# Transposing keys, gated outputs and probabilities from float32r copies in a hybrid GLA/attention encoder

## The chip, the cores and the metric

The kernel runs on one core of a Trainium2 chip. The metric is the time of one execution on the device, in microseconds (us). A core has five engines with a queue of instructions each: PE (TensorE, matrix products, whose weight loads are shown apart as PEld), DVE (VectorE), ACT (ScalarE), POOL (GpSimd) and SP (SyncE, which here only issues DMAs). Each engine works through its queue in order; they wait for each other through semaphores. A DMA is issued on the queue of an engine and then runs by itself.

## The reference

Two residual layers over 512 tokens of width 1024, in float32. Layer 0 mixes the tokens by gated linear attention (GLA), layer 1 by grouped-query softmax attention with rotary positions; each is followed by a gated MLP with a width-3 convolution. What matters here:

```python
# GLA, each of 4 heads, in both directions, in chunks of the tokens
kv_chunk = einsum('bhncd,bhncv->bhndv', k * exp(b_end - b), v)   # needs k with tokens on the contracted axis
...
o = rmsnorm(o, norm_w) * silu(g)                                  # the gated outputs
return o @ w_out
# attention, each of 8 query heads, in blocks of 128 queries
s = einsum('bkgqd,bksd->bkgqs', q_blk, k) * scale
p = softmax(s)                                                    # the probabilities
return einsum('bkgqs,bksd->bkgqd', p, v)                          # needs p with keys on the contracted axis
```

## The kernel before, in words

Activations are kept with features on the 128 partitions and the 512 tokens along them. Every large product is made of three products in float32r (`mm3`, L264 to L268): high part by high part, high by low, low by high. Both factors are split into a rounded float32r part (an ACT copy) and the rest (a DVE subtraction). Weights come as 1 MB tiles (`raw`, two buffers) on SP's queue, issued in `Weights.make` (L118), and are split there (L143, L144); a load waits until the tile two before it has been split.

The stages follow each other: GLA, MLP 0, attention, MLP 1. A tile framework puts the waits in, and a scheduler of its own orders the instructions on each engine, within what the program and the pools of buffers allow.

**GLA.** For each head h, `proj(h + 1)` (48 products of 512 columns) is written ahead of `core(h)`; after head 3's core there is none. `core(h)` does in order: `end`, the keys times a decay, for both directions (POOL, L482); their transposes by PE into the bank `kt`, three blocks of 128x128 a direction (L489), and an ACT copy into `kts` (L491); the products `in` (L501); the products `kv` of `kts` with `v` (L524), with ACT and DVE steps that chain them into states `sa` and `sb` (L525, L527); the outputs `o` (L548). Then ACT squares the outputs (L552, `junk`), DVE and POOL make a power of their sums (L198, L200, `ors`), and DVE multiplies outputs, this factor and the gate into the tiles `g` (L555). `tail(h)` transposes eight blocks of `g` by PE (L561, bank `tp`) and splits them into `oT` (L563, L564), the input of the output product `op` (L323). It is called inside the core of the next head; `tail(3)` comes after twelve steps of `op`.

**Attention.** 32 blocks (8 heads by 4 blocks of queries) go through a loop written out by hand: at step t it calls `scores(t)` (product `s`, its maximum, the exponential into a tile `p` of the tag "t", L784), then steps of generators that the lists `Q_STEPS`, `Q_READY` and `O_STEPS` assign to this t (projections of later query pairs, and the output product), then `turn(t - LAG)` (four transposes of `p` into the bank `pt`, L802, split into `pth` and `ptl`, L805 and L806), then `shares(t)` (`p` times the reciprocal of its sum, L789, L790), and every second step `mix` for the block `t - LAG2` (the products `po` with v, L266 to L268). LAG is 4 and LAG2 is 6. The banks for `s` are two, those for transposes (`pt`) are two, and the tag "t" has six buffers.

All transposes are `pe.transpose(out, in, ident)` with float32 tiles and a float32 identity.

Of the kernel before, what the change touches and what calls it, by code (L numbers as in the profile page):

```python
# [8 lines left out]
F32 = mybir.dt.float32  # L9
# [3 lines left out]
ALU = mybir.AluOpType  # L13
# [15 lines left out]

GATE_STEPS, GATE_LAG = (1, 3, 5, 7, 10, 12, 15, 17), 2  # L30

LAGS = (4, 6)

Q_STEPS = {1: (0, (4,) * 4), 2: (4, (3, 3, 2, 2, 2, 2, 2)), 3: (11, (2,) * 8)}
Q_READY = {1: (4, (3, 3, 2, 1, 1, 0, 1)), 2: (11, (3, 2, 2, 1, 1, 1, 0, 1)), 3: (19, (3, 2, 2, 1, 1, 1, 0, 1))}

O_STEPS = (22, 23, 25, 27, 29, 31, 32, 33, 34, 35, 36, 37)


PC_NORM = 0  # L40
# [6 lines left out]
def hybrid_encoder_kernel(  # L47
# [123 lines left out]
        sync.dma_start(raw[c // 4][:, r], w_vg[c // 4, :, r])  # L171
        W.raw[id(w_vg), c // 4] = raw[c // 4]

    ident = cp.tile([P, P], F32, name="ident")
    make_identity(nc, ident)

    two = tmp("u", "two")
    dve.memset(two[:, :P], 2.0 ** -5)
# [13 lines left out]
    def rsqrt_eps(src, w, n, scale=None, tag="tiny"):  # L192

        t = tiny(w, n, tag)
        if scale is None:
            dve.tensor_scalar(t, src, EPS, None, ALU.add)
        else:
            dve.tensor_scalar(t, src, scale, EPS, ALU.mult, ALU.add)  # L198
        r = tiny(w, n, tag)
        pool.tensor_tensor(r, t, halfneg[:, :w], ALU.pow)  # L200
        return r
# [141 lines left out]
    def gla(norm, nxt):  # L343
# [128 lines left out]

        def core(h, kqt, then):
            ends = big(F32, "end")
            ends = [ends[:, :S], ends[:, S:]]
            for d in range(2):
                e, f = EK[h, d], ends[d]
                dve.tensor_tensor(e[:, S:], e[:, S:], kqt[:, S:], ALU.mult)
                dve.tensor_tensor(e[:, :S], e[:, :S], kqt[:, :S], ALU.mult)
                sup = slice(0, 3) if d == 0 else slice(1, 4)  # L480
                v3 = lambda t: t.rearrange("p (s t) -> p s t", t=P)[:, sup, :]
                pool.tensor_tensor(v3(f), v3(e[:, S:]), FK[h, d][:, sup].rearrange("p (s o) -> p s o", o=1)  # L482
                                   .to_broadcast([P, 3, P]), ALU.mult)

            orders, keys = ([0, 1, 2], [3, 2, 1]), []
            for d, order in enumerate(orders):
                kt = bank("pt", "kt")
                for i, s in enumerate(order):
                    pe.transpose(kt[:, i * P : (i + 1) * P], ends[d][:, s * P : (s + 1) * P], ident)  # L489
                kts = tmp("t", "kts")  # L490
                act.activation(kts[:, : 3 * P], kt[:, : 3 * P], AF.Copy)  # L491
                keys.append(kts)

            at = tmp("t", "at")
            banks = []
            for d in range(2):
                e = EK[h, d]
                b = bank("acc" if h == GH - 1 else "s", "in")
                for s in range(NT):
                    o = s * P  # L500
                    mm(b[:, o : o + P], e[:, S + o : S + o + P], e[:, o : o + P], start=True, stop=True)  # L501
                banks.append(b)
            act.activation(at, banks[0], AF.Copy)

            def upper():
                dve.copy_predicated(at3, msk, banks[1].rearrange("p (s c) -> p s c", c=P))

            at3 = at.rearrange("p (s c) -> p s c", c=P)
            msk = smask.rearrange("p (o c) -> p o c", o=1).to_broadcast([P, NT, P])

            st = {}
            hs = slice(h * DV, (h + 1) * DV)
            for d, order in enumerate(orders):
                kts = keys[d]
                sa = tmp("t", "sa")
                sb = tmp("t", "sb") if d == 0 else st["b"]
                st["b"] = sb
                step = 1 if d == 0 else -1
                kv = bank("acc", "kv")
                kv2 = bank("po", "kv2")  # L520
                place = [kv[:, :DV], kv[:, DV:], kv2[:, :DV]]
                slot = [sa[:, :DV], sa[:, DV:], sb[:, d * DV : (d + 1) * DV]]
                for i, s in enumerate(order):
                    mm(place[i], kts[:, i * P : (i + 1) * P], v[s][:, hs], start=True, stop=True)  # L524
                act.activation(slot[0], place[0], AF.Copy)  # L525
                for i in (1, 2):
                    last = dve.scalar_tensor_tensor(slot[i], slot[i - 1], FK[h, d][:, order[i] : order[i] + 1],  # L527
                                                    place[i], ALU.mult, ALU.add)
                for i, s in enumerate(order):
                    st[d, s + step] = slot[i]  # L530
                if d == 0:
                    with tc.issue_after(last.ins) if h == GH - 1 else ExitStack():
                        upper()
            if then is not None:
                then()

            oss = tiny(4, "oss")
            og = []
            for s in range(NT):
                if s % 2 == 0:  # L540
                    bo = bank("s", "o")
                po = bo[:, (s % 2) * DV : (s % 2 + 1) * DV]
                parts = [(at[:, s * P : (s + 1) * P], v[s][:, hs])]
                for d in range(2):
                    if (d, s) in st:
                        parts.append((EK[h, d][:, s * P : (s + 1) * P], st[d, s]))
                for i, (l, r) in enumerate(parts):
                    mm(po, l, r, start=i == 0, stop=i == len(parts) - 1)  # L548
                og.append(po)
            for s in range(NT):  # L550
                junk = tmp("sq", "junk", DV)
                act.activation(junk, og[s], AF.Square, accum_out=oss[:, s : s + 1])  # L552
            ors = rsqrt_eps(oss, NT, "ors", 1.0 / DV)
            for s in range(NT):
                dve.scalar_tensor_tensor(g[s][:, hs], og[s], ors[:, s : s + 1], g[s][:, hs], ALU.mult, ALU.mult)  # L555

        def tail(h):
            for c in (2 * h, 2 * h + 1):
                tp = bank("pt", "tp")
                for s in range(NT):  # L560
                    pe.transpose(tp[:, s * P : (s + 1) * P], g[s][:, c * P : (c + 1) * P], ident)  # L561
                t = pair("xhl", 8, F32R, "oT")
                act.activation(t[:, :S], tp, AF.Copy)  # L563
                dve.tensor_tensor(t[:, S:], tp, t[:, :S].bitcast(F32), ALU.subtract)  # L564
                oh[c] = (t[:, :S], t[:, S:])
# [70 lines left out]
    def attention(norm, nxt):  # L636
# [90 lines left out]
        def qpair(i, tag="acc"):  # L727
            head, sc = yield from roped(1 + i, PC_QK, float(HD), "qsc", tag)
            for e in range(2):
                y = head(e)  # L730
                yield
                t = big(F32R, "q")
                split(y, t)
                heads[2 * i + e] = (t, sc, e)
                yield
# [51 lines left out]
        def shares(h, j):  # L787
# [2 lines left out]
            dve.tensor_scalar(p, p, rc, None, ALU.mult)  # L790
            probs[h, j] = p

        def turn(h, j):

            hf, i = divmod(j, 2)
            if i == 0:
                pts[h, hf] = tuple(big(F32R, n).rearrange("p (k q) -> p k q", q=256) for n in ("pth", "ptl"))
            ph3, pl3 = pts[h, hf]
            p = probs.pop((h, j))
            tp = bank("pt", "pt")  # L800
            for k in range(NT):
                pe.transpose(tp[:, k * P : (k + 1) * P], p[:, k * P : (k + 1) * P], ident)  # L802
            isl = slice(i * P, (i + 1) * P)
            tp3 = tp.rearrange("p (k q) -> p k q", q=P)
            act.activation(ph3[:, :, isl], tp3, AF.Copy)  # L805
            dve.tensor_tensor(pl3[:, :, isl], tp3, ph3[:, :, isl].bitcast(F32), ALU.subtract)  # L806
# [15 lines left out]
        LAG, LAG2 = LAGS  # L822
        blocks = [(h, j) for h in range(QH) for j in range(NT)]
        osteps = out_steps(w_aout, oh, nxt)
        plan = collections.defaultdict(list)
        for i in range(1, QH // 2):
            g = qpair(i)
            for first, counts in (Q_STEPS[i], Q_READY[i]):
                for t, n in enumerate(counts):
                    plan[first + t] += [g] * n  # L830
        for t in O_STEPS:
            plan[t].append(osteps)
        for t in range(len(blocks) + LAG2):
            if t < len(blocks):
                scores(*blocks[t])
            for g in plan[t]:
                next(g, None)
            if LAG <= t < len(blocks) + LAG:
                turn(*blocks[t - LAG])
            if t < len(blocks):  # L840
                shares(*blocks[t])
            if t >= LAG2:
                h, j = blocks[t - LAG2]
                if j % 2 == 1:
                    mix(h, j // 2)
# [88 lines left out]
```

## Time and profile before

| | |
|---|---|
| time, median of 3 runs | 1133.47 us (1133.27 to 1133.87) |
| time of the profiled execution | 1133.16 us |
| its span, first to last instruction | 1131.4 us |
| PE busy | 1125.7 us, 99% |
| DVE, ACT, POOL busy | 690.1, 482.1, 76.0 us |
| HBM read and written | 100.34 MB, 2.10 MB |
| transposes of `pt`, `tp`, `kt` | 128, 32, 24 |

A row of a group names the line, the engine, the operation, output and inputs, the shape and the count; behind the bar stand the busy time of all and the mean duration of one in ns, then the idle time ahead of them. A row of the timeline begins with the start and the length in us, and one of the chain of waits' pieces likewise. A row of the waits names who waited for whom, the total in us, how often, and the longest. A row of one tile gives the shortest, middle and longest duration in ns. A row of a window gives its length, then the busy time of PE, PEld, DVE, ACT and POOL, the granted PE clock, the share of the DMA engines and GB/s. A row of a DMA gives the count, the size and the median us from issue to landing.

### The profile page before, as it was taken

To read this page: it belongs to the slowest core of one execution; us is meant where nothing else is said; L and a number is where in the kernel's file an instruction comes from. 1 tells how busy PE (TensorE), PEld (TensorE's weight loads), DVE (VectorE), ACT (ScalarE), POOL (GpSimd) and SP (SyncE) were. 2 spreads that over 40 slices of the span, in tenths; PEclk is the share of its full clock that TensorE was granted. 3 is DMA by queue.
4 is the path that set the end of the run, shared out by engine and by line. 5 is a ranking of instruction groups with operands and counts; after the bars stand their busy time and mean duration, and the time that the engine had idled before them with its cause. 6 is when DMAs were issued, how large, how long until landed. Compare 5 with 4: busy or idle time off the path is not lost.

```text
span 1131.4 us, 12991 instructions
## 1 busy us (share of the span) xinstructions
PE 1125.7 (99%) x5260; PEld 939.2 (83%) x5260; DVE 690.1 (61%) x996; ACT 482.1 (43%) x690; POOL 76.0 (7%) x66
## 2 busy tenths in 40 slices
PE   9999999999999999999999999999999999999998
PEld 7888888888888888888888888888888888888887
DVE  6787563677777777633325589766777777762221
ACT  5564232444444444422234667644444444442210
POOL 0104110000000000000004433000000000000000
PEclk9999999999999999999999999999999999999999
DMA  6422211232322323223247633223232232323320
GB/s 231 149 75 78 84 63 38 75 112 75 112 97 90 112 75 112 100 86 112 77 152 181 149 76 75 56 75 112 75 112 85 101 112 75 112 84 121 130 93 19
DMA packets 19980, 111.66 MB, mean 99 GB/s; under 512 B 2384, under 2 KB 3024, under 8 KB 8400
## 3 DMA queue, kind: packets, MB, share of 16 engines
q1 hardware_dynamic: 17328, 102.29, 25.9%
q0 software_dynamic: 2304, 8.39, 3.9%
q8 instruction: 41, 0.67, 0.2%
q10 hardware_dynamic: 288, 0.15, 0.0%
q14 instruction: 19, 0.16, 0.0%
HBM read 100.34 MB, written 2.10 MB: 91 GB/s over the span
## 4 chain that ended last, share of the span: by engine, by line
PE 99%; DVE 0%; DMA 0%; ACT 0%; issue 0%; SPq 0%; DVEq 0%; ACTq 0%
PE up L266 14%; PE up L267 14%; PE up L268 14%; PE vg L297 8%; PE op L323 8%; PE dn L266 7%; PE dn L268 7%; PE dn L267 7%; PE o L548 2%; PE pt L802 1%; PE av L297 1%; PE kv L524 1%; PE A L266 1%; PE A L268 1%; PE A L267 1%; PE B L266 1%
## 5 line engine op out<-in xcount | busy, mean ns | idle before, releaser
L143 ACT ACTIVATE wh<-raw 128x1024 fp32r<-128x1024 f32 x164 | 173.3, 1056 | 351.4 <-PE up L267 132.8
L144 DVE TENSOR_TENSOR wl<-raw,wh 128x1024 fp32r<-128x1024 f32 x164 | 203.7, 1242 | 144.8 <-ACT wh L143 144.6
L266 PE MATMUL up<-xhl,wh 128*128 128x512 f32 x704 | 274.3, 390 | 0.0
L268 PE MATMUL up<-xhl,wl 128*128 128x512 f32 x704 | 273.9, 389 | 0.0
L267 PE MATMUL up<-xhl,wh 128*128 128x512 f32 x704 | 273.9, 389 | 0.0
L268 PEld LDWEIGHTS up<-xhl,wl 128*128 128x128 f32 x704 | 132.2, 188 | 27.6
L266 PEld LDWEIGHTS up<-xhl,wh 128*128 128x128 f32 x704 | 132.2, 188 | 27.4
L267 PEld LDWEIGHTS up<-xhl,wh 128*128 128x128 f32 x704 | 132.2, 188 | 27.1
L266 PE MATMUL dn<-gu,wh 128*128 128x512 f32 x352 | 136.9, 389 | 0.0
L267 PE MATMUL dn<-gu,wh 128*128 128x512 f32 x352 | 136.9, 389 | 0.0
L268 PE MATMUL dn<-gu,wl 128*128 128x512 f32 x352 | 136.9, 389 | 0.0
L603 DVE TENSOR_TENSOR u<-up,R 128x512 f32<-128x512 f32 x88 | 60.3, 687 | 52.7 <-PE up L268 52.7
L297 PE MATMUL vg<-wh,xhl 128*128 128x512 f32 x256 | 79.7, 390 | 0.6 <-DVE halfneg L184 0.6
L605 ACT ACTIVATE y<-u,cw 128x512 f32<-128x512 f32 x88 | 71.2, 811 | 20.4 <-DVE u L603 20.4
L268 PEld LDWEIGHTS dn<-gu,wl 128*128 128x128 f32 x352 | 66.1, 188 | 13.8
L267 PEld LDWEIGHTS dn<-gu,wh 128*128 128x128 f32 x352 | 66.1, 188 | 13.7
L266 PEld LDWEIGHTS dn<-gu,wh 128*128 128x128 f32 x352 | 66.1, 188 | 13.6
L323 PE MATMUL op<-oT,wh 128*128 128x512 f32 x256 | 70.9, 395 | 0.0
L607 DVE SCALAR_TENSOR_TENSOR y<-u,cw,y 128x511 f32<-128x511 f32 x88 | 65.9, 751 | 2.9
L606 DVE SCALAR_TENSOR_TENSOR y<-u,cw,y 128x511 f32<-128x511 f32 x88 | 65.6, 746 | 0.6 <-ACT y L605 0.6
L609 ACT ACTIVATE y<-y 128x512 f32<-128x512 f32 x44 | 27.9, 634 | 87.8 <-DVE y L607 87.8
L297 PEld LDWEIGHTS vg<-wh,xhl 128*128 128x128 f32 x256 | 48.0, 188 | 10.6 <-ACT sq L240 0.7
(186 smaller groups left out, 1432.1 us busy)
## 6 DMA issues: line engine op xcount, KB each, us to landing
raw<-in_w_up_dram SPq DMA_DIRECT2D x44, 1024.0 KB, 4.8
raw<-in_w_down_dram SPq DMA_DIRECT2D x22, 1024.0 KB, 4.8
wl<-raw POOLq DMA_DIRECT2D x16, 512.0 KB, 4.7
raw<-in_w_vg_dram SPq DMA_DIRECT2D x6, 1024.0 KB, 4.7
raw<-in_w_akq_dram SPq DMA_DIRECT2D x5, 1024.0 KB, 5.2
raw<-in_w_kq_dram SPq DMA_DIRECT2D x4, 1024.0 KB, 4.8
raw<-in_w_gout_dram SPq DMA_DIRECT2D x4, 1024.0 KB, 4.8
raw<-in_w_aout_dram SPq DMA_DIRECT2D x4, 1024.0 KB, 4.9
```

The source lines that it names most:

```text
L143: act.activation(hi[:, sl], r[:, sl], AF.Copy)
L144: dve.tensor_tensor(lo[:, sl], r[:, sl], hi[:, sl].bitcast(F32), ALU.subtract)
L266: mm(ps, wh, mh, start=start, stop=False)
L267: mm(ps, wh, ml, start=False, stop=False)
L268: mm(ps, wl, mh, start=False, stop=stop)
L297: mm(ps[j][:, :width], hl[k][i == 2][:, j * P : (j + 1) * P], (wl if i == 1 else wh)[:, sl], start=k == 0 and i == 0, stop=k == KC - 1 and ...
L323: mm(pss[ng][n], wt[:, sl], mv, start=k == 0 and i == 0, stop=k == KC - 1 and i == 2)
L603: dve.tensor_tensor(u, ps, norm.R, ALU.mult)
L605: act.activation(y, u, AF.Identity, scale=w(1), bias=w(3))
L606: dve.scalar_tensor_tensor(y[:, 1:], u[:, : S - 1], w(0), y[:, 1:], ALU.mult, ALU.add)
L607: dve.scalar_tensor_tensor(y[:, : S - 1], u[:, 1:], w(2), y[:, : S - 1], ALU.mult, ALU.add)
L609: act.activation(res[1], res[1], AF.Silu)
```

## The change

The three groups of transposes read float32r tiles, with a float32r identity, into the same banks seen as float32r. Since the compiler lets only certain writers fill a float32r tile, each tile is filled by a DMA that copies the float32 words as they are (the destination is seen as float32):

- keys: two copies of 128x384 a head, from `end` into new tiles `ew` of the tag "u", on SP's queue, in `core`;
- gated outputs: the gate writes a new tile `gated` (128x1024) instead of `g`; one copy a head from it into a tile `gw`, on SP's queue, at the end of `core`; `tail` transposes from `gw`;
- probabilities: a new function `copy`, one copy of 128x512 a block from `p` into a tile `pr` of the tag "t", on ACT's queue, called at step t for block t - 1, after `scores(t)`.

The identity is made in a scratch tile and copied by DVE into the float32r tile. In attention LAG becomes 5 and LAG2 7, the first step of each query pair's generator is called ahead of `scores` at the steps of `Q_FIRST`, and the lists move a few steps.

```diff
-LAGS = (4, 6)
+LAGS = (5, 7)
-Q_READY = {1: (4, (3, 3, 2, 1, 1, 0, 1)), 2: (11, (3, 2, 2, 1, 1, 1, 0, 1)), 3: (19, (3, 2, 2, 1, 1, 1, 0, 1))}
-O_STEPS = (22, 23, 25, 27, 29, 31, 32, 33, 34, 35, 36, 37)
+Q_READY = {1: (4, (3, 3, 2, 0, 1, 0, 1)), 2: (11, (3, 2, 2, 1, 0, 1, 0, 1)), 3: (19, (3, 2, 2, 1, 0, 1, 0, 1))}
+Q_FIRST = {1: 7, 2: 15, 3: 23}
+O_STEPS = (22, 23, 25, 27, 29, 31, 32, 34, 35, 36, 37, 38)
...
-    ident = cp.tile([P, P], F32, name="ident")
-    make_identity(nc, ident)
+    eye = tmp("sq", "eye")[:, :P]
+    make_identity(nc, eye)
+    identr = cp.tile([P, P], F32R, name="ident")
+    dve.tensor_copy(identr, eye)
+    ident = identr.bitcast(F32)
...
+                t = sp.tile([P, S], F32R, tag="u", bufs=4, name=nm("ew"))
+                cols = slice(sup.start * P, sup.stop * P)
+                sync.dma_start(t.bitcast(F32)[:, cols], f[:, cols])
+                words.append(t)
...
-                    pe.transpose(kt[:, i * P : (i + 1) * P], ends[d][:, s * P : (s + 1) * P], ident)
+                    pe.transpose(kt[:, i * P : (i + 1) * P].bitcast(F32R), words[d][:, s * P : (s + 1) * P], identr)
...
+            gated = big(F32, "gated")
             for s in range(NT):
-                dve.scalar_tensor_tensor(g[s][:, hs], og[s], ors[:, s : s + 1], g[s][:, hs], ALU.mult, ALU.mult)
+                dve.scalar_tensor_tensor(gated[:, s * DV : (s + 1) * DV], og[s], ors[:, s : s + 1], g[s][:, hs],
+                                         ALU.mult, ALU.mult)
+            t = big(F32R, "gw")
+            sync.dma_start(t.bitcast(F32), gated)
+            gws[h] = t
...
-                    pe.transpose(tp[:, s * P : (s + 1) * P], g[s][:, c * P : (c + 1) * P], ident)
+                    o = s * DV + (c % 2) * P
+                    pe.transpose(tp[:, s * P : (s + 1) * P].bitcast(F32R), gw[:, o : o + P], identr)
...
+        def copy(h, j):
+            t = sp.tile([P, S], F32R, tag="t", bufs=6, name=nm("pr"))
+            act.dma_start(t.bitcast(F32), probs[h, j])
+            probs[h, j] = t
...
-                pe.transpose(tp[:, k * P : (k + 1) * P], p[:, k * P : (k + 1) * P], ident)
+                pe.transpose(tp[:, k * P : (k + 1) * P].bitcast(F32R), p[:, k * P : (k + 1) * P], identr)
...
+            if t in ahead:
+                next(ahead[t])
             if t < len(blocks):
                 scores(*blocks[t])
+            if 1 <= t <= len(blocks):
+                copy(*blocks[t - 1])
```

In the built program SP issues, from head 0 on: keys (two copies), a load of output weights, gated outputs of head 0; keys, load, gated outputs of head 1; keys, load, gated outputs of head 2; keys, gated outputs of head 3, load. In head 3 PE has the `in` products ahead of the key transposes, where before they stood behind them.

More of the change, by code (lines that the diff above doesn't have):

```diff
@@ L474, in core @@
             ends = big(F32, "end")
-            ends = [ends[:, :S], ends[:, S:]]
+            ends, words = [ends[:, :S], ends[:, S:]], []
             for d in range(2):
@@ L553, in core @@
             ors = rsqrt_eps(oss, NT, "ors", 1.0 / DV)
+            gated = big(F32, "gated")
             for s in range(NT):
-                dve.scalar_tensor_tensor(g[s][:, hs], og[s], ors[:, s : s + 1], g[s][:, hs], ALU.mult, ALU.mult)
+                dve.scalar_tensor_tensor(gated[:, s * DV : (s + 1) * DV], og[s], ors[:, s : s + 1], g[s][:, hs],
[3 more added lines that the diff above has]
+            gws[h] = t
+        gws = {}
         def tail(h):
+            gw = gws.pop(h)
             for c in (2 * h, 2 * h + 1):
@@ L824, in attention @@
         osteps = out_steps(w_aout, oh, nxt)
-        plan = collections.defaultdict(list)
+        plan, ahead = collections.defaultdict(list), {}
         for i in range(1, QH // 2):
             g = qpair(i)
+            ahead[Q_FIRST[i]] = g
             for first, counts in (Q_STEPS[i], Q_READY[i]):
```

## The prediction

> **What bounds the kernel now.** I read the page from the top. Part 1 gives the busy shares, part 4 the chain that ended last, part 2 the granted clock.
>
> ```profile
> span 1131.4 us, 12991 instructions
> PE 1125.7 (99%) x5260; PEld 939.2 (83%) x5260; DVE 690.1 (61%) x996; ACT 482.1 (43%) x690; POOL 76.0 (7%) x66
> PEclk9999999999999999999999999999999999999999
> PE 99%; DVE 0%; DMA 0%; ACT 0%; issue 0%; SPq 0%; DVEq 0%; ACTq 0%
> ```
>
> PE is busy for 99% of the span, it is 99% of the chain, and its clock is full throughout. Since a busy PE need not be at its peak, the waits of PE come next: all three that there are.
>
> ```profile
> PE warm L182 <- DVE bd L188: 1.3, 1, 1.3
> PE vg L297 <- DVE halfneg L184: 0.6, 1, 0.6
> PE s L266 <- ACT p L784: 0.3, 1, 0.3
> ```
>
> Two of them belong to the start, the warming products and the first weights. So any time taken off PE's instructions is gained, and any hole that the change tears into PE's stream is lost; nothing else counts. The profiled execution took 1133.16 us with a span of 1131.4, so 1.76 us lie around it; the median of the runs is 1133.47. I make the sum on 1133.16 and add 0.3 at the end.
>
> **Part 1: 184 transposes in float32r.** The diff touches three groups, and the rows give their counts: 128 of probabilities, 32 of gated outputs, 24 of keys.
>
> ```profile
> L802 PE MATMUL pt<-ident,p x128: 270/272/309, 643.8 to 734.2; 128*128 128x128 f32 x128
> L561 PE MATMUL tp<-ident,g x32: 270/273/273, 146.3 to 201.1; 128*128 128x128 f32 x32
> L489 PE MATMUL kt<-ident,end x24: 270/272/273, 121.3 to 174.1; 128*128 128x128 f32 x24
> 200.37 1.03 PE L561 MATMUL tp<-ident,g 128*128 128x128 f32 x8
> 184.18 16.35 PE op L323 x72
> 614.09 11.52 PE av L297 x96
> ```
>
> The 272 ns are a latency; what PE pays is the distance between starts. Eight in a row take 1.03 us, the last of them 0.273, so one step is (1.03-0.273)/7 = 108 ns. The chain rows give the float32r step: 16.35/72 = 227 ns for 512 columns, 11.52/96 = 120 for 256. The difference is 107 ns for 256 columns, 0.42 a column, with 13 fixed. A float32r transpose of 128 columns would so take 53+13 = 67 ns, against 0.84 a column now. No row shows a float32r operation of 128 columns. From below, the 53 ns of its columns plus the 2 ns that the float32 step has over 0.84 a column: 55. From above, whatever bounds the loading of weights:
>
> ```profile
> L802 PEld LDWEIGHTS pt<-ident,p 128*128 128x128 f32 x128 | 16.1, 141 | 4.0
> L297 PEld LDWEIGHTS av<-wh,xhl 128*128 128x128 f32 x64 | 9.9, 189 | 0.0
> 666.87 0.97 PEld L652 LDWEIGHTS hs<-bd,qa 128*128 128x128 f32 x8 [0.24 <-DVE qa L667]
> ```
>
> In the tiny products of L652, with two columns, only the loads count: (0.97-0.19)/7 = 111 ns a step, for loads of 190 ns like the float32r ones. The loads of today's transposes last 141, some 50 ns less, so they may step at about 60. I take 67 ns, nearest to the float32r rows: 184 x (108-67) = **-7.5 us**, 5.2 of it in attention and 2.3 in GLA. The ends are -9.8 (55 ns) and +0.6 (111 ns).
>
> The Trainium skill ("TensorE: Matmul & The Clock Gate", section "LDWEIGHTS (loading the stationary operand)") gives a load as its columns over 1.2, an estimated 107 ns here, and its next section has no fast load for float32. That speaks against the change: by it the term is -0.2 us (184 x 1 ns) in place of -7.5. The 111 ns of L652 agree; the 141 ns loads of the transposes do not. It is the first rival below.
>
> **Part 2: the last GLA head.** In the built order of the changed kernel, SyncE issues for each head the two copies of keys, then a weight load, then the copy of gated outputs. So the keys of head 3 stand behind the gated outputs of head 2, on an in-order queue. The key transposes of head 3 follow head 2's outputs on PE at once; no projection lies between them, as one does in heads 1 and 2. The old rows there:
>
> ```profile
> 159.41 0.83 POOL L482 TENSOR_TENSOR end<-ek,fk 128x384 f32<-128x384 f32 x1 [3.28 <-DVE ek L478]
> 161.18 1.74 POOL L482 TENSOR_TENSOR end<-ek,fk 128x384 f32<-128x384 f32 x1 [0.94 <-DVE ek L478]
> 173.50 0.82 PE L489 MATMUL kt<-ident,end 128*128 128x128 f32 x6
> 173.77 0.39 ACT L552 ACTIVATE junk<-o 128x256 f32<-128x256 f32 x1 [1.32 <-PE o L548]
> 174.16 1.95 PE L501 MATMUL in<-ek 128*128 128x128 f32 x16
> 174.64 0.17 DVE L198 TENSOR_SCALAR ors<-oss 128x4 f32<-128x4 f32 x1 [3.77 <-ACT junk L552]
> 174.89 1.01 POOL L200 TENSOR_TENSOR ors<-ors,halfneg 128x4 f32<-128x4 f32 x1 [11.97 <-DVE ors L198]
> 175.93 1.66 DVE L555 SCALAR_TENSOR_TENSOR g<-o,ors,g 128x256 f32<-128x256 f32 x4 [1.12 <-POOL ors L200]
> 174.50 0.87 ACT L491 ACTIVATE kts<-kt 128x384 f32<-128x384 f32 x2
> 175.95 2.32 PE L524 MATMUL kv<-v,kts 128*128 128x256 f32 x10
> 178.08 0.48 DVE L527 SCALAR_TENSOR_TENSOR sb<-sa,fk,kv 128x256 f32<-128x256 f32 x1
> 178.62 0.70 PE L524 MATMUL kv<-v,kts 128*128 128x256 f32 x2
> out_dram<-x SPq DMA_DIRECT2D x7, 256.0 KB, 2.1
> out_dram<-x SPq DMA_DIRECT2D x1, 128.0 KB, 1.7
> wl<-raw POOLq DMA_DIRECT2D x16, 512.0 KB, 4.7
> ```
>
> Head 3's keys were ready at 162.9 (161.18+1.74), so nothing waited at 173.50. In the changed order POOL makes them after head 2's power, which costs 1.7 us more but is done by 177.6, no later than the gate. The new chain, on the old clock: outputs finished, squares 173.77, power to 175.90, gate to 177.59, copy of gated outputs issued at 177.65, keys 0.35 later. The store rows give 1.7 us for 128 KB and 2.1 for 256, that is 1.3 fixed and 0.4 for each 128 KB. The 512 KB of gated outputs land at 177.65+2.9 = 180.55, and 192 KB of keys behind them 0.6 later, at 181.15. PE meanwhile has the `in` products (from 174.16 to 175.95, 16 steps in 1.79 us, now from 173.50 to 175.29) and then nothing: **5.85 us idle**. From below, keys that pass the big copy land at 178.0+1.9 = 179.9: 4.6 idle. From above, if copies inside SBUF go like the row of `wl`, 4.7 us for 512 KB, the keys land at about 183: 7.7 idle.
>
> Two smaller losses follow, since `in` no longer covers them. Between key transposes and `kv` lies an ACT copy, half of the 0.87 us, with its hops: about 0.6. The last `kv` of a head waits for `sb`: it began at 178.62, 2.67 after the first, though the five before it take 2.16 (ten steps of 216 ns). Transposes of gated outputs filled that; now they all stand behind it: 0.5. Together 1.1 and so **+6.9 us** for the hole (5.7 to 8.8). On SyncE the two key copies wait behind the gated outputs, and after the next gate a load of output weights:
>
> ```profile
> 186.44 1.66 DVE L555 SCALAR_TENSOR_TENSOR g<-o,ors,g 128x256 f32<-128x256 f32 x4 [1.12 <-POOL ors L200]
> 191.58 0.33 SPq L118 DMA_DIRECT2D raw<-in_w_gout_dram  x1
> ```
>
> It was issued at 191.58, when its buffer came free; the gate of head 3 ended at 188.1, and both shift with PE, so this load loses nothing. Heads 0 to 2 have cover: 48 projection products of 227 ns stand before their transposes, and the copies are issued beside them.
>
> **Part 3: the clock after the hole.** The trace has one more stretch without PE work, its end.
>
> ```profile
> 1127.40 0.39 PE L268 MATMUL dn<-gu,wl 128*128 128x512 f32 x1
> 1129.00:1131.40 2.40, 0.00 (x0) 0.00 (x0) 0.00 (x0) 0.00 (x0) 0.00 (x0) 0.91 0.33 109
> 1.27 3.62 PE L182 MATMUL warm<-two 128*128 128x128 f32 x16 [1.27 <-DVE bd L188]
> ```
>
> In the last 2.4 us the granted clock averages 0.91: it fell before the end, at most 3.6 us after the last product. At the start the 16 warming products take 3.62/16 = 226 ns each, twice the 112 of the same shape in `in`: half clock, for some 3.4 us. A hole of 5.85 us is long enough for such a fall; 3.4 us of work at half clock lose 1.7. I take **+1.7** (0 to 3.4). The Trainium skill (same page, "Part 1: The HAM clock gate") has the clock halved after an idle window of about 3.4 us, free-running; the end of this trace agrees, within 3.6 us.
>
> **Part 4: attention.** 32 copies of 256 KB go to ACT's queue, each waiting at most for the one before to land (2.1 us by the store row) or for a tile that a transpose frees. Behind a waiting copy stand the next exponential and the copy out of `pt`, and PE waits for both.
>
> ```profile
> L784 ACT ACTIVATE p<-s,nb,qsc x32: 761/778/787, 629.9 to 726.5; 128x512 f32<-128x512 f32 x32
> 1128.61 0.36 ACTq L633 DMA_DIRECT2D out_dram<-x  x1
> 680.00:720.00 40.00, 39.74 (x247) 33.84 (x245) 34.73 (x82) 28.25 (x55) 9.72 (x8) 1.00 0.30 68
> ```
>
> A block takes (726.5-629.9)/31 = 3.1 us, in the dense stretch somewhat less. There DVE is busy 34.73 of 40 us (87%), ACT 28.25 (71%). An issue costs ACT 0.36 us, 12% of a block, so ACT goes to 83%; PE gets 0.16 us a block faster, so DVE goes to some 92%. Neither becomes the bound by itself, but two in-order engines this full, each waiting for the other, give part of the gain back: **+1.5**, between 0 and the whole 5.2. The fifth block of lag covers the landing: four blocks, over 11 us, against 2.1. The lists of steps move work and add none. The identity's extra copy on DVE comes while PE multiplies, long before its first use, in `rows`, after the first segment: nothing, or about the 0.17 us of the small DVE row above if it held the products up.
>
> **The sum.** -7.5 +6.9 +1.7 +1.5 = +2.6 us: 1133.16+2.6 = 1135.8, on the median's scale 1136.1.
>
> **Rivals.** *Transposes bound by their loads.* At 108 to 111 ns nothing is gained and the holes stay, with 1.0 in attention: 0 to 0.6, 6.9, 1.7, 1.0 give 9.6 to 10.2, about 1143. For it: the 111 ns step, and no float32r row under 256 columns. Against it: the loads of 141 ns.
>
> *The keys pass the gated outputs* (faster). If head 3's keys land at 179.9, the hole is 5.7 in all and the clock may hold; with 55 ns and nothing lost in attention the time is 1133.47-9.8+5.7 = 1129.4. At 67 ns it is 1131.7. It decides from a hole, with what the clock takes, under 7.5 less attention's 1.5: 6.0 us. For it: the 16 engines are nearly idle there.
>
> ```profile
> DMA  6422211232322323223247633223232232323320
> ```
>
> The seventh slice, 170 to 198 us, has a digit of 1, a busy share of some 10%. Against it: it is one queue, and 4.6 us are idle even then.
>
> *Attention bound by ACT's queue.* If the copies' landings pace the exponentials, the whole 5.2 is lost: 1139.7. Against it: 2.1 us of landing against 2.9 a block.
>
> **How the numbers follow.** The forecast has 0.50, loads 0.25, keys that pass 0.20, ACT's queue 0.05. The forecast's own range is 1131.5 to 1139.5. The range of all is 1129 to 1143.5. About 0.2%, 2.3 us, is what a measurement of this kernel can tell from no change. Slower by more: 0.25 of the forecast, the loads and ACT's queue, 0.55. Within: 0.20 of the forecast, 0.05 of passing keys, 0.25. Faster: 0.05 of the forecast, 0.15 of passing keys, 0.20.
>
> **What would show it.** Steps of `pt` near 67 ns; a PE wait of 5 to 6 us at the key transposes, near 175, released by a DMA of `ew`; granted clock under 1 in the 3 us behind it; small PE waits for ACT between 640 and 740. Wrong would be: steps of 108 ns or more, no wait for `ew`, or PE waiting for ACT for more than 5 us.

## The result, and the profile after

The changed kernel takes 1142.59 us (median of 4 runs, 1142.11 to 1142.89). The kernel before took 1133.67 us beside it (4 runs). The ratio is 1.0079, 95% interval 1.0066 to 1.0091: 8.9 us slower.

First the head of the page of the changed kernel, as it was read of the kernel before: span, busy shares, then the digits of PE and of its clock in 40 slices.

```profile
span 1141.1 us, 13128 instructions
PE 1127.1 (99%) x5260; PEld 938.6 (82%) x5260; DVE 690.5 (61%) x997; ACT 481.3 (42%) x690; POOL 75.0 (7%) x66
PE   9999997999999999999999999999999999999998
PEclk9999998999999999999999999999999999999999
```

PE is still busy for 99%, and that share alone would say that nothing happened. The digits say where to look: in the seventh slice PE falls to 7 and its clock to 8. Next the waits of PE in the changed kernel (who waited for whom, total us, how often, longest).

```profile
PE kt L499 <- DMA ew<-end: 5.7, 1, 5.7
PE s L272 <- ACT q L720: 1.5, 1, 1.5
PE warm L188 <- DVE bd L194: 1.3, 1, 1.3
PE s L272 <- ACT p L803: 1.0, 2, 0.8
PE op L329 <- DVE oT L721: 0.3, 1, 0.3
```

One new wait of 5.7 us is in the last GLA head, for the copied keys. Two new ones of more than half a microsecond, 1.5 and 0.8 us, are in attention. Here is the timeline of the first, on all engines, in the changed kernel (start, length, engine, what, and the idle time ahead with its releaser).

```profile
173.72 1.95 PE L511 MATMUL in<-ek 128*128 128x128 f32 x16
176.08 1.61 POOL L488 TENSOR_TENSOR end<-ek,fk 128x384 f32<-128x384 f32 x2
176.14 1.66 DVE L566 SCALAR_TENSOR_TENSOR gated<-o,ors,g 128x256 f32<-128x256 f32 x4 [1.12 <-POOL ors L206]
177.83 0.47 SPq L569 DMA_DIRECT2D gw<-gated  x1
178.39 1.38 SPq L492 DMA_DIRECT2D ew<-end  x2
181.38 1.15 PE L499 MATMUL kt<-ident,ew 128*128 128x128 f32 x6 [5.71 <-DMA ew<-end]
182.55 5.49 PE L534 MATMUL kv<-v,kts 128*128 128x256 f32 x12
187.48 1.24 PE L580 MATMUL tp<-ident,gw 128*128 128x128 f32 x8
```

Two orders make the keys late. POOL, which made head 3's keys at 159.41 and 161.18 before, now makes them at 176.08, behind the power of head 2 (`ors`). It finished the first half within about 0.8 us, but SP did not issue their copy before 178.39: it stood behind the copy of head 2's gated outputs, which the gate released at 177.80. By an estimate from these rows, SP's order alone held the first copy for at most 1.5 us (176.9 to 178.39); POOL's order and the landing are the rest of the wait. PE ran out of `in` products at 175.67 and stood until 181.38. The twelve `kv` then took 5.49 us, where ten of them had taken 2.32. The windows show why (length, busy time of PE, PEld, DVE, ACT, POOL, then the granted clock):

```profile
175.70:181.30 5.60, 0.00 (x0) 0.00 (x0) 1.66 (x4) 0.00 (x0) 1.99 (x3) 0.69 0.42 161
181.40:188.00 6.60, 6.58 (x20) 5.04 (x20) 1.96 (x4) 2.24 (x5) 0.00 (x0) 0.50 0.02 4
188.00:191.00 3.00, 3.00 (x21) 2.71 (x20) 1.89 (x4) 1.09 (x2) 0.00 (x0) 0.99 0.00 0
```

For 6.6 us behind the hole PE worked at half clock.

**Where the 8.9 us are.** I take the stages between starts that both traces have. From the first key transpose to attention's first product `s`: 625.45 - 121.30 = 504.14 us before, 634.05 - 121.96 = 512.09 after, **+7.95** for GLA (MLP 0, in between, is untouched). From the first `s` to the last `po`: 114.38 before, 115.15 after, **+0.77** for attention. Of the 9.7 us between the two spans 1.0 remain: 0.66 lie ahead of the first key transpose, whose start varied from 120.89 to 121.96 between the profiled executions of kernels with nearly the same work up to there, and 0.3 behind attention. So nearly all of it is one place, and attention, which was to gain, gained nothing.

### The profile page after: what moved, and what is told of

It is laid out like the page before. It is cut to its first block, busy times and chain, and to the rows that moved or that the text cites. A ratio compares the mean times of both kernels' runs of the same rounds, so it can differ in the third digit from the quotient of the medians.

```text
span 1141.1 us, 13128 instructions
## 1 busy us (share of the span) xinstructions
PE 1127.1 (99%) x5260; PEld 938.6 (82%) x5260; DVE 690.5 (61%) x997; ACT 481.3 (42%) x690; POOL 75.0 (7%) x66
```

## The experiments

The theory, formed on these two traces: (a) the hole in head 3 costs its wait and then half a clock; (b) a float32r transpose gains much less than forecast; (c) in attention the copies take back what the transposes gain. The rivals are written with each run. A time is a median; the ratio is to the kernel before on the same chip, with its 95% interval.

**1. The GLA part alone.** Attention's lists, copies and transposes are put back.

```diff
-LAGS = (5, 7)
+LAGS = (4, 6)
...
-            if 1 <= t <= len(blocks):
-                copy(*blocks[t - 1])
```

> The change's GLA part alone; attention is as in the kernel before. My theory after the two traces: the whole loss is made in the last GLA head, by 5.7 us of TensorE waiting for the key copy behind the gated-output copy, and by about 2.5 us more of TensorE at half clock behind the wait; the 56 copied transposes of the other steps give back about 1 us. That is 1133.7 + 8 = about 1142, and the offset at attention's first product against the kernel before is +8 us. Rival (attention's copies, on ScalarE's queue, cost most): about 1135 here. Rival (the half clock costs nothing that counts): about 1139.

1141.35 us, ratio 1.0068 (1.0053 to 1.0083). The GLA part has nearly the whole loss, and its trace has the same single wait of 5.7 us for `ew`.

**2. The attention part alone.** Keys and gated outputs are transposed in float32 from `end` and `g`, without copies.

```diff
-                t = sp.tile([P, S], F32R, tag="u", bufs=4, name=nm("ew"))
-                sync.dma_start(t.bitcast(F32)[:, cols], f[:, cols])
...
-            sync.dma_start(t.bitcast(F32), gated)
```

> The change's attention part alone (probabilities copied, transposed as float32r, five blocks behind); keys and gated outputs are transposed as before. My theory: the 128 transposes gain about 20 ns each, 2.5 us, and the waits for the copies take back that and a little more: 1133.5 to 1135, with no wait of TensorE over 2 us anywhere. Rival (attention's copies cost most of the change's loss): about 1141. Rival (the transposes gain 41 ns each, and the waits seen in the changed kernel come from GLA's delay): about 1129.

1134.43 us, ratio 1.0009 (0.9999 to 1.0018): no gain, and no loss that can be told from none. The rival with 41 ns a transpose (1129) is out, and so is the one with ScalarE's queue as the main cost. The two parts add up: 7.9 and 1.0 us over their reference, 8.8 with roundings, against 8.9 for the whole.

**3. The last head's keys early.** The keys and their copies become a function of their own, `prep`. For head 3 it is called ahead of head 2's core, so that POOL makes them ahead of head 2's power and SP issues them ahead of the gated outputs. In the traces DVE's order is the same and ACT's nearly so; about a dozen of PE's instructions move.

```diff
-            core(h, kqt, (lambda: tail(h - 1)) if h else None)
+            mine = words if h == GH - 1 else prep(h, kqt)
+            if h == GH - 2:
+                words = prep(h + 1, nxtk)
+            core(h, mine, (lambda: tail(h - 1)) if h else None)
```

> The whole change, but the last head's keys and their copies are written ahead of the head before's core, so that on SyncE's queue the key copy no longer stands behind the gated-output copy. My theory: TensorE's wait for the key copy, 5.7 us in the changed kernel, goes, and with it the fall of the clock and its 2.5 us: about 1134, from 1133.3 to 1135. Rival (the clock falls at this place whatever the wait is, since the short transposes are thin work): about 1137. Rival (another wait takes the place, the gated outputs' own copy): 1138 to 1142.

1133.33 us, ratio 0.9999 (0.9990 to 1.0009). Having head 3's keys made and copied early is worth 9 us. POOL makes them where it did in the kernel before:

```profile
159.38 0.83 POOL L488 TENSOR_TENSOR end<-ek,fk 128x384 f32<-128x384 f32 x1 [3.21 <-DVE ek L484]
161.25 1.74 POOL L488 TENSOR_TENSOR end<-ek,fk 128x384 f32<-128x384 f32 x1 [1.04 <-DVE ek L484]
```

The last of their copies is issued at 163.0. The edit moves POOL's order and SP's together, and no run moved one of them alone; how the 9 us divide between them is not shown. In PE's timeline nothing is left of the hole:

```profile
173.21 0.82 PE L501 MATMUL kt<-ident,ew 128*128 128x128 f32 x6
173.86 2.02 PE L513 MATMUL in<-ek 128*128 128x128 f32 x16
175.71 2.32 PE L536 MATMUL kv<-v,kts 128*128 128x256 f32 x10
```

and in its window there the granted clock (the third number from the end) is full:

```profile
175.00:182.00 7.00, 6.86 (x39) 5.40 (x39) 4.37 (x10) 2.50 (x6) 0.78 (x1) 1.00 0.20 78
```

**4. The hole filled.** The whole change, with 25 products that feed nothing where PE waits.

```diff
+                if h == GH - 1 and d == 0:
+                    for _ in range(25):
+                        mm(kt, norm.hl[0][0][:, :P], norm.hl[1][0], start=True, stop=True)
```

> The whole change with 25 discarded 128x512 products in float32r between the last head's first products and its key transposes, the place where TensorE waits 5.7 us in the changed kernel; results are unchanged. The wait is filled with work that feeds nothing. My theory: the copy still lands when it did, so the 5.7 us stay, but the granted clock stays near 1 behind it, and the time falls by the clock's share alone, some 2.5 us: about 1140. Rival (the clock's share is nothing): 1142.6, as the change. Rival (the products run past the landing): up to 1143.

1140.04 us, ratio 1.0058 (1.0041 to 1.0075). The keys still land late, and the filling products end before they do. PE's timeline:

```profile
172.81 6.04 PE L500 MATMUL kt<-xhl,xhl 128*128 128x512 f32 x25
178.69 1.72 PE L514 MATMUL in<-ek 128*128 128x128 f32 x14
180.56 0.45 PE L502 MATMUL kt<-ident,ew 128*128 128x128 f32 x3 [0.15 <-DMA ew<-end]
```

The window behind it, in which the change had a clock of 0.50, has a full one:

```profile
182.00:185.00 3.00, 2.93 (x18) 2.40 (x16) 1.72 (x4) 1.40 (x4) 0.00 (x0) 1.00 0.03 8
```

With the stage of above (first key transpose to attention's first product), three runs split the 7.95 us. Early keys: 625.12 - 121.62 = 503.50, which is -0.64 against before: what the 56 GLA transposes gain, less anything that the copies cost in that stage. Hole filled: 630.68 - 121.23 = 509.45, so the hole without the clock costs +5.95. The change: 512.09, so the clock costs +2.64. In the run of GLA alone it is 632.90 - 121.35 = 511.55 and so 2.1: there the clock came back sooner. Each stage is read from one profiled execution, and the filler puts two of the `in` products between the key transposes, so 5.95 and 2.64 are good to a few tenths.

**5 and 6. The step of a transpose, by itself.** 200 discarded transposes of the identity, ten in each of 20 steps of MLP 0; once in float32r, once in float32 (without the `bitcast`, with `ident`).

```diff
+            if layer == 0 and m >= 2:
+                ex = bank("po", "ex")
+                for n in range(10):
+                    i = n % 4
+                    pe.transpose(ex[:, i * P : (i + 1) * P].bitcast(F32R), identr, identr)
```

> The whole change with 200 more transposes of the identity, in float32, ten in each of 20 steps of the first MLP layer, where TensorE does nothing but multiply; they go to an idle bank and are discarded. It measures the step of a float32 transpose among products. By the 108 ns of eight in a row: 200 x 108 = 21.7 us over the change, about 1164.3, and starts 108 ns apart in the trace. A step bound by the loads (111 ns) would give the same within 0.6 us.

> As its twin in float32, but the 200 discarded transposes are in float32r. By the prediction's 67 ns: 13.4 us over the change, 1156.0. My theory now, from the changed kernel's groups of four (weight loads some 85 ns apart, 92 a transpose with the ends): 17 to 18.4 us, about 1160. By the prediction's rival (111 ns, the loads): 22.2 us, 1164.8, as in float32.

Medians 1168.92 (1164.33 to 1170.21) and 1164.78 us (1160.48 to 1166.54), ratios 1.0299 (1.0274 to 1.0323) and 1.0264 (1.0238 to 1.0289). Both profiled executions have a wait in attention that the changed kernel hasn't: 4.6 and 4.4 us, products of scores waiting for an exponential (its cause is below). So the step is read from the place itself. The ten in float32, and the next product:

```profile
271.46 1.25 PE L621 MATMUL ex<-ident 128*128 128x128 f32 x10
272.47 0.48 PE L272 MATMUL up<-xhl,wh 128*128 128x512 f32 x1
```

and the same in float32r:

```profile
270.58 0.98 PE L621 MATMUL ex<-ident 128*128 128x128 f32 x10
271.39 0.46 PE L272 MATMUL up<-xhl,wh 128*128 128x512 f32 x1
```

The last of each ten is taken at its duration, 0.25 us in float32r and 0.27 in float32; in the first, this is the row of the line (shortest, middle, longest, in ns):

```profile
L621 PE MATMUL ex<-ident x200: 221/251/253, 270.6 to 495.5; 128*128 128x128 f32 x100
```

In float32r a step is (0.98-0.25)/9 = **81 ns**, in float32 (1.25-0.27)/9 = **109 ns**. Over the stage from the first MLP product to attention's first the 200 cost 419.63 - 396.67 = 22.96 us in float32 and 415.08 - 396.67 = 18.41 in float32r: 115 and 92 ns each, with the ends, a gain of 23. Neither 67 nor 111 holds.

The 81 ns are a mean of unlike steps. By the medians of the 20 rows, the starts in the trace lie 108 to 109 ns apart throughout in float32, but in float32r the first two steps are 56 and 67 ns and the others 86 to 88. The end of a row differs too: the next product starts 28 ns after the last float32 transpose, but 86 ns after the last float32r one. The rows above show the ends as 0.03 and 0.08 us between the start of the last transpose and that of `up`.

**7 and 8. Attention taken apart.** GLA as before. Once only the lag and the lists, transposes straight from `p`; once with the copies as well, transposed in float32.

```diff
-                pe.transpose(tp[:, k * P : (k + 1) * P].bitcast(F32R), p[:, k * P : (k + 1) * P], identr)
+                pe.transpose(tp[:, k * P : (k + 1) * P], p[:, k * P : (k + 1) * P].bitcast(F32), ident)
```

> GLA as in the kernel before; of attention's part only the order: five blocks of lag and the changed lists of steps, with float32 transposes straight from the probabilities and no copies. My theory: the order by itself costs nothing, 1133.5 within 0.7. Rival (the longer lag holds up buffers that ScalarE needs): 1135 to 1136, with TensorE waiting for ScalarE.

> As the run with the order alone, and the probabilities are copied as in the change, but transposed in float32 from the copies. It holds the copies' cost without the faster transposes. The attention part as a whole gave 1134.4. My theory (transposes gain 2 to 2.5 us there, the copies cost some 3): about 1137. Rival (the copies cost 1 us, the float32r transposes gain nothing): about 1134.5. Rival (float32 transposes leave ScalarE the slack to hide the copies, so the wait only appears with the faster step): 1133.5.

1135.96 us, ratio 1.0019 (1.0009 to 1.0028), and 1141.04 us, ratio 1.0064 (1.0047 to 1.0081). Both are slower than I expected. The order alone is not free: it brought PE a wait for DVE that the kernel before has not.

```profile
PE hs L660 <- DVE nb L790: 1.0, 1, 1.0
```

The copies on top cost 5.1 us, and float32r on top of that gains 6.6 (1141.04 to 1134.43). But 128 transposes by 23 ns are 2.9 us. I put the rest down to the order, though no run shows it: the scheduler sets every engine's order when the kernel is built, and between these two builds, which differ in the type of one operand, 239 of PE's 5260 products stand at another place in the trace. These runs compare orders as well as costs, and I cannot take them as a clean split.

**9 and 10. Tiles of their own for the copies.** In the changed kernel `p` and its copy come from the same six tiles of the tag "t". In the built program a copy mostly goes into a tile that one of the last copies, often the one just before, has read, so it waits for that landing, and on ACT everything behind it waits too. Here two blocks share a tile of the large pool instead, once with early keys, once with GLA as before.

```diff
-            t = sp.tile([P, S], F32R, tag="t", bufs=6, name=nm("pr"))
+            hf, i = divmod(j, 2)
+            if i == 0:
+                prs[h, hf] = big(F32R, "pr")
+            t = prs[h, hf][:, i * S : (i + 1) * S]
```

> The whole change with the last head's keys copied early (which gave 1133.3), and the copied probabilities in tiles of their own, two blocks to a tile of the large pool, in place of the pool of six that the probabilities themselves use. In the built program a copy then no longer waits for the copy before it to land. My theory: the two stalls of 1.2 us in which products of scores wait for an exponential, and that waits 5.9 us for a copy, come from this sharing; they go, and with them some 2.5 us: 1130.3 to 1131.3, with a sum of stalls of TensorE in attention of about 1 us (3.6 before). Rival (ScalarE's issue time and DVE's load make the stalls): 1133. Rival (the weight load that shares the engines with the copy delays whatever waits next): 1132 to 1133.

> The attention part alone (which gave 1134.4), with the copied probabilities in tiles of their own. My theory: 1131.5 to 1132.3, faster than the kernel before by the 3.5 us that 128 transposes gain at 81 in place of 108 ns, less what ScalarE's and DVE's order still costs (1 to 2 us). Rival (the sharing has no part in it): 1134.4.

1138.00 us, ratio 1.0040 (1.0027 to 1.0052), and 1138.49 us, ratio 1.0044 (1.0032 to 1.0057). My theory of what these tiles would bring fell. Half of it held: the tile view of `pr` lists who waited for a copy. With early keys and shared tiles:

```profile
who waited for it (us, times):
  ACT pth L835: 11.2, 12
  ACT p L808: 7.3, 2
  ACT wh L125: 1.9, 1
```

and with tiles of their own, where the exponentials are gone from the list:

```profile
who waited for it (us, times):
  ACT pth L838: 8.6, 7
  PEld pt L835: 1.1, 3
```

But the freed tiles gave the scheduler another order (259 of PE's 5260 products at another place in the trace), and that order stalls between 700 and 730 in many short waits: PE is busy for 26.05 of 30 us there, against 29.70 with shared tiles, and its clock falls for a while (0.94 over the stretch). The windows of that stretch, first with shared tiles:

```profile
700.00:730.00 30.00, 29.70 (x188) 24.73 (x188) 25.13 (x62) 19.98 (x41) 4.89 (x4) 1.00 0.44 136
```

then with tiles of their own:

```profile
700.00:730.00 30.00, 26.05 (x148) 20.26 (x147) 21.65 (x55) 18.37 (x38) 1.47 (x2) 0.94 0.44 141
```

ACT's exponentials, which no longer waited for copies, waited for DVE's maxima instead: 26.8 us in attention, where it was 11.8 with shared tiles. The row of ACT's waits:

```profile
ACT p L808 <- DVE nb L806: 26.8, 23, 2.6
```

**11. The old order with it.** As run 9, with the lag and lists of the kernel before.

> As the run with tiles of their own and early keys, but with the four blocks of lag and the lists of steps of the kernel before. The order alone, without copies, cost 2.4 us. Theory A (that cost belongs to the order as such): 2 us under its twin. Theory B (it is one wait that another spacing of TensorE and ScalarE makes or removes): the same as its twin, within 0.7. Theory C (the shorter lag now makes transposes wait for copies): 1 to 2 us over its twin.

1138.70 us (1135.16 to 1140.34), ratio 1.0053 (1.0039 to 1.0067). The median is within 0.7 of its twin, as theory B has it, but single runs lie 5 us apart, more than the differences in question; it settles nothing. The time goes with the granted clock: 1135.16 at 1.000, 1138.43 and 1138.70 at 0.998, 1140.13 and 1140.34 at 0.997. So part of the spread is the clock's. What one order costs with other tiles stays open, since no run held the order fixed.

**12. The version to keep.** Early keys, gated outputs and keys in float32r, attention as before.

> The GLA part with the last head's keys early, attention as before. 56 transposes gain 19 to 27 ns each, 1.1 to 1.5 us, and no wait stands against it: 1132.0 to 1132.5. Rival (the copies bring small waits elsewhere in GLA): 1133.5 or more.

1132.86 us, ratio 0.9996 (0.9987 to 1.0004). The stage of GLA is 624.72 - 121.26 = 503.45, 0.7 us shorter than before, where 56 transposes by 23 ns would be 1.3; where the rest goes no run shows. Over the whole kernel the gain cannot be told from no change. No version that I ran is measurably faster than the kernel before.

## Why the prediction was right in its direction, and where its terms were off

The time lies outside the forecast's own range, 1131.5 to 1139.5, and within the range of all the rivals, 1129 to 1143.5.

| term | forecast, us | measured, us | from |
|---|---|---|---|
| transposes in attention | -5.2 | -2.0 | 61 ns a group of four, taken for all 32 |
| transposes in GLA | -2.3 | -0.6 | early keys against before |
| hole in head 3 | +6.9 | +5.95 | hole filled against early keys |
| clock behind it | +1.7 | +2.6 (2.1 in GLA alone) | change against hole filled |
| attention's queues | +1.5 | +2.7 | a remainder: +0.77 in all, less the -2.0 |
| sum | +2.6 | +8.7 | result: +8.9 |

**The hole** was right in place, mechanism and size of the wait: 5.85 us forecast, 5.71 in the trace. The prediction had both orders, SP's queue and POOL's keys behind head 2's power. The landing, forecast for 181.15, released PE at 181.38. Only the 1.1 us of side losses were too much: all that was lost without the clock is 5.95. The rival in which the keys pass the gated outputs is out.

**The clock** was right as a mechanism and short in size. I had taken 3.4 us of work at half clock from the start of the trace; the windows show 6.6 us (181.4 to 188.0), and in the run of GLA alone 5.1:

```profile
180.70:185.80 5.10, 5.03 (x15) 4.03 (x16) 1.25 (x3) 1.85 (x4) 0.00 (x0) 0.51 0.01 3
```

The Trainium skill ("TensorE: Matmul & The Clock Gate", section "Part 1: The HAM clock gate") has a free-running window of about 3.4 us, so that the time to recover depends on where in it the work begins; 6.6 and 5.1 us lie above one window and below two, which agrees with waiting for the first window that is busy throughout. Finer windows agree: in the change the clock was low from 177.8 (0.91 from 177 to 178) to 188.06 (0.84 from 188.0 to 188.2), 10.2 us or three times 3.4, and in GLA alone from 178.9 to 185.7 (0.94 from 178 to 179, 0.79 from 185.5 to 186), or twice 3.4. But the fall did not need a whole idle window: in the change it came 2.1 us after PE had stopped.

**The transposes** are the largest mis-sized term: -7.5 us forecast, -2.6 measured. Two steps of the prediction failed. The first is the line through the float32r rows of 256 and 512 columns, drawn on to 128: "A float32r transpose of 128 columns would so take 53+13 = 67 ns". Only the first two steps of a row are that short; from the third on they take 86 to 88, and a row of ten has a mean of 81 ns. The second is the multiplication, 184 x (108-67), which gives every transpose a whole step and puts the end of a group at nothing. In attention the groups are of four, one before and one after:

```profile
643.85 0.60 PE L802 MATMUL pt<-ident,p 128*128 128x128 f32 x4
655.03 0.46 PE L827 MATMUL pt<-ident,pr 128*128 128x128 f32 x4
```

Less the last one's duration (0.27 and 0.25), three steps take 0.33 us and then 0.21: 109 and 70 ns each, close to the forecast. But the step from the last transpose to the next product, 28 ns before, is 85 after (medians). So a group gains some 115 ns inside and loses 57 at its end. From the start of the product before a group to that of the product behind it, the median is 586 ns before and 525 after: 61 ns for four, 15 a transpose where I had 41, and 32 x 61 ns = 2.0 us. The reason to doubt the line stood in the prediction, as its rival: with so few columns something else bounds the step. But its 111 ns was as wrong. The rule of the Trainium skill behind it (same page, "LDWEIGHTS (loading the stationary operand)", an estimated 107 ns) isn't borne out by 81 ns. What does set these steps no run here shows.

This rival gave 1143, and the result is 1142.6. That is a coincidence of sums: its transposes were to gain nothing (they gain 2.6 us), its attention was to lose 1.0 (2.7), its clock 1.7 (2.6). A total that fits is no evidence for the terms.

In **attention** one step failed outright: "The fifth block of lag covers the landing: four blocks, over 11 us, against 2.1." It looks only at the transposes, which are the readers of the copy. They are not the first to wait for the landing. The next copy and the exponential behind it on ACT need the tile that the copy reads, about one block later. The timeline of ACT and SP in the changed kernel:

```profile
650.76 45.98 SPq L120 DMA_DIRECT2D raw<-in_w_aout_dram  x3
651.27 0.77 ACT L803 ACTIVATE p<-s,nb,qsc 128x512 f32<-128x512 f32 x1
651.34 0.47 ACTq L815 DMA_DIRECT2D pr<-p  x1
657.82 0.78 ACT L803 ACTIVATE p<-s,nb,qsc 128x512 f32<-128x512 f32 x1 [5.69 <-DMA pr<-p]
657.87 0.47 ACTq L815 DMA_DIRECT2D pr<-p  x1
```

A copy issued at 651.34, 0.58 us behind a weight load of 1 MB, held the next exponential until 657.82, and PE's `s` at 658.74 waited 0.80 us for it. The second number that failed is the 2.1 us of landing, which was read from the stores at the end of the kernel. The tile view of `pr` gives 2.2, 2.4 and 6.9 us as shortest, middle and longest:

```profile
DMA to landing us min/median/max: 2.2/2.4/6.9
```

The window of the long one:

```profile
650.80:657.80 7.00, 7.00 (x41) 5.90 (x39) 4.37 (x8) 1.33 (x3) 5.99 (x5) 1.00 0.87 226
```

In those 7 us the DMA engines are 87% busy with the load, the parts of `wl` and the copy. In the two runs with extra transposes the same copy, issued 0.6 us behind the same load, held the exponential for 9.5 and 9.3 us, and PE for 4.6 and 4.4. Why the same meeting costs 5.7 us in one build and 9.5 in another is open. ACT's own issue was 0.47 us a copy, not 0.36.

This landing cost PE 0.8 us. The longer wait of attention in the changed kernel is of another kind:

```profile
689.59 0.50 PE L272 MATMUL s<-k,q 128*128 128x512 f32 x1 [1.55 <-ACT q L720]
```

POOL had finished `ry`, from which ACT makes this `q`, at 687.56. ACT began `q` at 688.91, behind a `pth`, the issue of a copy (0.47 us) and an `oT`. That is ACT's full queue, which the prediction had as a mechanism.

That the sharing of tiles makes ACT wait is shown by its end with tiles of their own (run 9). What it costs PE over the 0.8 us is not shown: undoing it changed the order too. The 2.7 us of the table are a remainder, and these two waits make 2.3 of them.

## What to carry to other kernels

Before a DMA is added to an in-order queue, list what already stands there, when its source is made, and which engine needs each landing first: here the last head's keys were made and copied behind the head before's outputs, with no projection to cover them. That cost all of the 8.9 us, and doing both earlier gave it back. A buffer that a copy reads is in use until the copy has landed, so the first to wait may be the next writer, not the reader that the lag was made for. And a step for a shape that no row shows should be measured among real neighbours, ends included, before it is multiplied by 184: groups of four gained 15 ns a transpose where the line gave 41.

## What the runs showed of the hardware that was not expected

In a row of ten at full clock float32r transposes of 128x128 step at 81 ns on average (56, 67, then 86 to 88), float32 ones at 109; the median latencies are 251 and 272 ns. A product behind them starts 86 ns after the last float32r transpose and 28 ns after the last float32 one. The clock also falls without a long hole: in the run with tiles of their own, whose longest single wait of PE in that stretch is under 1 us, the granted clock was 0.85 and 0.72 in two successive windows of 4 us. That is half clock from 714.8 to 718.2, and in the 3.4 us ahead PE was busy for 2.09.

```profile
711.40:714.80 3.40, 2.09 (x11) 1.17 (x9) 2.48 (x7) 2.98 (x7) 0.36 (x1) 1.00 0.87 202
712.00:716.00 4.00, 2.79 (x13) 1.72 (x14) 3.68 (x10) 3.13 (x8) 0.00 (x0) 0.85 1.02 252
716.00:720.00 4.00, 4.00 (x21) 3.47 (x21) 2.56 (x8) 1.85 (x4) 0.00 (x0) 0.72 0.80 242
```
